# Rows of the attention mix loaded during the sample turns, into tiles of their own and into the places of cached keys

## The chip, the cores and the metric

One core of one Trainium2 chip runs the whole kernel. The metric is device time in microseconds (us) of one execution; smaller is better. The median of three runs of the kernel before is 1789.62 us (1786.05 to 1790.71).

## The reference

One layer of a streaming encoder, for a prompt of 1024 rows (T) and a sample of 64 rows (S) that share the weights; the width is 1024. Cut to what matters here:

```
h  = rms_norm(x, g_norm1);  q, k, v, forget logits = h @ w_in        # 16 heads: 8 of kind A, 8 of kind B
oa, ob = attend(prompt heads), attend(sample heads with cached k, v)
x  = x + concatenate([oa, ob]) @ w_o                                 # the "mix" times w_o
mk, mv = memory keys and values = rms_norm(mem) @ w_mkv
x  = x + attend(rms_norm(x) @ w_mq, mk, mv) @ w_mo
x  = x + conv_ffn(rms_norm(x))                                       # w_up, conv, silu, w_down
```

Products run as three products of parts: each f32 operand is split into a high part (`hi`, a cast on ScalarE) and a low part (`lo`, the difference, on VectorE or GpSimd), and hi\*hi, lo\*hi and hi\*lo are summed in PSUM.

## The kernel before, in words

**Prompt attention.** Heads go in pairs, eight of them. Each finished block of 256 query rows of a pair is written to the DRAM tensor `mixd` (eight rows of 128 x 1024, one for each pair; 512 KB each). The last of these writes goes out at 601 us.

**Memory and sample, beside each other.** The list `line` holds pieces of the memory product (L679, 24 matmuls for one half of a column block; weights `mwraw` are loaded by L661 and split by L668/L669 into `mwhi` and `mwlo`). Between its pieces stand the sample's eight turns, one for each pair of heads, in the order SAMPLES = 4, 7, 5, 6, 0, 1, 3, 2. A turn of a pair consists of:
- `load`: queries and new keys `sqd` (L727), values `svn` (L729), the bias `s`, two tiles of cached keys `kraw` (L740, three places in all) and of cached values `vraw`;
- `prep`: four transposes on TensorE (L754), from which ScalarE and VectorE make queries `sq` and new keys `skn` (L265 and L266, two each, by turns);
- `splitk`: `kchi` (L774, ScalarE) and `kclo` (L775, VectorE);
- `score`: matmuls L797 (cached keys) and L798 (new keys), then VectorE adds the bias and takes the largest value (L800, L802, L807), ScalarE takes the exponential (L808), VectorE the reciprocal of the sum (L810);
- `turn` and `sum`: transposes of the probabilities (L822), split into `pth` (L823) and `ptl` (L824), and ten products with the values (L835);
- the end: two halves `st` (L842, ScalarE) and `su` (L843, VectorE), a transpose of `su` (L847), and two copies into `smix` (L849).

The turns overlap: the loads, `prep` and `splitk` of the next turn stand beside the score of this one and the sums of the last one. The list PER says how many memory pieces go with each turn. The last two turns are those of pair 3 (the seventh) and of pair 2 (the eighth).

**Output projection.** After the seventh turn the memory pieces are used up, and `open_left` opens new pools on the left side: `raw`, `hi` and `lo` for the weights w_o (loads L911, splits L919 and L920), and `ha`, the eight rows of the mix as parts. Row k is loaded into `mraw` (L976), cast on ScalarE (L979) and differenced on VectorE (L980); the sample's columns come from `smix` (L1022, L1023). A pool `stage` has four places for `mraw`: four rows are loaded at once, and the split of row k loads row k + 4. The product with w_o (L937) takes the rows in order, k = 0 to 7, three matmuls each; the first two products (chunks of 384 columns into `pj`) share the first weight tiles, and the third begins with `PT`.

**What sets the order.** The program is written as one list of steps (`weave` puts small steps between large ones), but the compiler of the tile framework then orders each engine's instructions by its own planning. Engines execute their queues strictly in that order. All DMAs are issued by SyncE's queue (SP), in order too: a load that waits for its place holds up all those behind it.

Of the kernel before, what the change touches and what calls it, by code (L numbers as in the profile page):

```python
# [7 lines left out]
F32 = mybir.dt.float32  # L8
F32R = mybir.dt.float32r
ACT = mybir.ActivationFunctionType  # L10
ALU = mybir.AluOpType
# [4 lines left out]
P = 128  # L16
T = 1024
# [3 lines left out]
KT = 8  # L21
# [4 lines left out]
SLOW = 7  # L26
LEFT = (0, 0, 0, 15)
PER = (4, 8, 9, 12, 6, 5, 6, 0, 0)
STAGE, MIXES = 4, 8
WARM = 20  # L30
EPS = 1e-6
NEG = -1e30
# [9 lines left out]
def hybrid_step(ctx: ExitStack, tc: tile.TileContext, i: dict, o: dict):  # L42
    nc = tc.nc
    act, dve, pool, pe = nc.scalar, nc.vector, nc.gpsimd, nc.tensor

    def f32(ap):
        return ap.bitcast(F32)
# [17 lines left out]
    mixd = dram.tile([8, P, T], F32, name="mixd")  # L65
# [38 lines left out]
    left = ExitStack()  # L104
# [540 lines left out]
    left = ExitStack()  # L645
# [241 lines left out]
    rest = ExitStack()  # L887
# [2 lines left out]
    zq = [mq.tile([P, 4, S], F32R, name=f"sq{x}") for x in range(2)]  # L890
    for x in range(2):
        pool.memset(f32(zq[x][:, 1:3]), 0.0)
    samples = [Sample(p) for p in SAMPLES]
    samples[0].load()
    step(0, [samples[0].prep, lambda: samples[0].splitk(0), lambda: samples[0].splitk(1)])
# [59 lines left out]
    mixr = []  # L955
# [6 lines left out]
    def open_left():  # L962
        nonlocal stream
        left.close()
        stream = Stream(late_left.enter_context(tc.tile_pool(name="wr", bufs=1, side="left")))
        x = late_left.enter_context(tc.tile_pool(name="x0", bufs=1, side="left")).tile([P, 384], F32, name="x0")
        nc.sync.dma_start(x, i["xT"][0, :, 0:384])
        ha = mixes.enter_context(tc.tile_pool(name="ha", bufs=1, side="left"))
        stage = rest.enter_context(tc.tile_pool(name="stage", bufs=1, side="left"))
        mixr.extend(parts(ha, "a"))  # L970
        stream.fetch()
        raws = {}

        def load_mix(k):
            raws[k] = stage.tile([P, T], F32, name="mraw", bufs=STAGE)
            nc.sync.dma_start(raws[k], mixd[k])  # L976

        def split_mix(k):
            act.copy(mixr[0][k][:, 0:T], raws[k])  # L979
            dve.tensor_tensor(mixr[1][k][:, 0:T], raws[k], f32(mixr[0][k][:, 0:T]), op=ALU.subtract)  # L980

        for k in range(STAGE):
            load_mix(k)

        def split_load(k):
            split_mix(k)
            if k + STAGE < KT:
                load_mix(k + STAGE)

        return ha, [lambda k=k: split_load(k) for k in range(KT)], x  # L990

    old, mixes_todo, ha = [], [], None
    todo = first[:]
    for x in range(len(samples) + 1):
        if not line and ha is None:
            ha, mixes_todo, early_x = open_left()
        cur = samples[x] if x < len(samples) else None
        nxt = samples[x + 1] if x + 1 < len(samples) else None
        if nxt:
            nxt.load()  # L1000
        new, fin = [], []
        if cur:
            new = [cur.score, cur.splitv]
        if nxt:
            fin = [nxt.prep, lambda: nxt.splitk(0), lambda: nxt.splitk(1)]
        subs = new[:1] + old[:2] + new[1:] + old[2:-1] + fin[:1] + old[-1:] + fin[1:]
        main = line[:PER[x]]
        del line[:PER[x]]
        if ha and not mixes_todo:
            stream.upto(4)  # L1010
            if todo:
                main = todo.pop(0).pieces
        subs += mixes_todo[:MIXES]
        del mixes_todo[:MIXES]
        weave(main, subs)
        if cur:
            c = cur.nc
            old = [lambda z=z, u=cur: u.turn(z) for z in range(2)] + [lambda u=cur: u.sum(0)]
            old += ([lambda u=cur: u.turn(2), lambda u=cur: u.sum(1)] if c == 2 else [])
            old += [lambda u=cur, c=c: u.sum(c), cur.out]  # L1020
# [844 lines left out]
```

## Time and profile before

| what | value |
|---|---|
| median of three runs | 1789.62 us (1786.05 to 1790.71) |
| the profiled execution, its own time | 1791.44 us |
| its span, first to last instruction | 1789.7 us |
| TensorE (PE) busy | 1717.8 us, 96% |
| VectorE (DVE), ScalarE (ACT), GpSimd (POOL) busy | 1208.6, 937.0, 644.7 us |
| mean DMA rate over the span | 112 GB/s |
| chain that ended last, in TensorE | 49% of the span in its largest groups |

Times in the profile count from the first instruction. PE is the matmuls, PEld the weight loads beside them, SPq the queue of SyncE. A row of the timeline gives the start, the duration (for "x3" of three together), the engine, the line, what is written from what, and in brackets the idle time of that engine before it with the one that ended it. A row of the stages gives the stage, its length, the busy time of each engine with its count, the granted TensorE clock as a share of full speed, the share of DMA engines in use, and GB/s.

### The profile page before, as it was taken

The page shows a single profiled execution, that of the slowest core. Times are in us where ns is not written, and L with a number is a line of the kernel's source. Part 1 is how long each engine was busy: PE and PEld are TensorE (multiplying, and loading weights), DVE is VectorE, ACT ScalarE, POOL GpSimd, SP SyncE. Part 2 cuts the span into 40 slices and gives each one's busy share as a digit, 9 for nine tenths or more (in the row PEclk, how much of TensorE's full clock was granted, in tenths as well). Part 3 has the DMA queues.
Part 4 walks back from the last instruction along what each step waited for, and adds up shares of the span by engine and source line. Part 5 has one row for each costly group of instructions (what it writes and reads, how often), then busy time and mean ns, then how long its engine had stood idle before and what let it go on. Part 6 is the DMA issues. An engine that isn't in the chain of part 4 may idle for free.

```text
span 1789.7 us, 33957 instructions
## 1 busy us (share of the span) xinstructions
PE 1717.8 (96%) x12432; PEld 1667.2 (93%) x12432; DVE 1208.6 (68%) x2642; ACT 937.0 (52%) x2058; POOL 644.7 (36%) x931
## 2 busy tenths in 40 slices
PE   7898999999997898999999999999999999999999
PEld 6888999999997787999999999999999999999999
DVE  5767667677677777433444379877777777677994
ACT  6756666677677577334545455433333333433332
POOL 4656657878777443453433612000000000000000
PEclk8999999999999999999999999999999999999999
DMA  7322122122113677441111563222222222884232
GB/s 248 98 63 66 57 73 80 51 73 75 47 56 106 203 248 234 155 144 54 54 48 57 165 204 102 79 76 87 83 87 74 73 73 73 272 296 158 77 118 80
DMA packets 134247, 199.87 MB, mean 112 GB/s; under 512 B 20968, under 2 KB 74088, under 8 KB 134080
## 3 DMA queue, kind: packets, MB, share of 16 engines
q1 hardware_dynamic: 134080, 197.70, 34.9%
q8 instruction: 98, 1.61, 0.4%
q14 instruction: 69, 0.57, 0.1%
HBM read 155.35 MB, written 45.44 MB: 112 GB/s over the span
## 4 chain that ended last, share of the span: by engine, by line
PE 49%; DVE 2%; issue 1%; POOL 1%; DMA 1%; ACT 0%; SPq 0%; POOLq 0%; ACTq 0%; DVEq 0%
PE W L1449 25%; PE W L1746 12%; PE pj L937 7%; PE W L937 1%; PE S L1192 1%; PE tq L1228 1%; PE O L1228 1%; POOL lo L920 1%; DMA kvraw<-in_w_down_dram 1%; PE PT L1215 0%; DMA f<-x2d 0%; PE O L1192 0%; PE PT L1173 0%; POOL s L1207 0%; ACT hi L919 0%
## 5 line engine op out<-in xcount | busy, mean ns | idle before, releaser
L299 PE MATMUL pj<-whi,xhi 128*128 128x384 f32 (+1 forms) x512 | 195.5, 382 | 2.7 <-DVE flog L314 1.6
L299 PE MATMUL pj<-wlo,xhi 128*128 128x384 f32 (+1 forms) x512 | 176.4, 344 | 4.5 <-POOL wlo L123 4.5
L299 PE MATMUL pj<-whi,xlo 128*128 128x384 f32 (+1 forms) x512 | 175.2, 343 | 0.6 <-DVE xlo L131 0.6
L1555 POOL COPY s<-gp 128x2 f32<-128x2 f32 x22 | 15.8, 718 | 335.8 <-DVE gp L1554 335.8
L1449 PE MATMUL W<-h,hi 128*128 128x272 f32 x704 | 134.4, 288 | 1.4 <-ACT qlo L1585 1.4
L504 ACT ACTIVATE s<-s,mx 128x640 f32<-128x640 f32 (+7 forms) x128 | 94.4, 737 | 77.6 <-DVE mx L502 76.7
L1746 PE MATMUL W<-f,hi 128*128 128x272 f32 x672 | 127.6, 287 | 3.6 <-DVE f L1314 2.3
L541 DVE TENSOR_TENSOR ptl<-PT,pth 128x512 fp32r<-128x512 f32 (+2 forms) x192 | 99.5, 522 | 38.5 <-ACT pth L540 36.2
L1449 PEld LDWEIGHTS W<-h,hi 128*128 128x128 f32 x704 | 110.8, 188 | 1.7 <-ACT qlo L1585 1.6
L1746 PEld LDWEIGHTS W<-f,hi 128*128 128x128 f32 x672 | 105.3, 188 | 4.4 <-DVE f L1314 2.5
L540 ACT CAST pth<-PT 128x512 fp32r<-128x512 f32 (+2 forms) x192 | 84.7, 448 | 43.9 <-PE PT L539 42.3
L299 PEld LDWEIGHTS pj<-wlo,xhi 128*128 128x128 f32 x512 | 99.2, 194 | 6.3 <-POOL wlo L123 6.1
L299 PEld LDWEIGHTS pj<-whi,xhi 128*128 128x128 f32 x512 | 98.8, 193 | 4.8 <-DVE flog L314 1.9
L1449 PE MATMUL W<-h,lo 128*128 128x272 f32 x352 | 101.8, 289 | 0.0
L1313 ACT CAST hi<-raw 128x512 fp32r<-128x512 f32 x68 | 42.2, 621 | 109.5 <-PE W L1449 59.2
L299 PEld LDWEIGHTS pj<-whi,xlo 128*128 128x128 f32 x512 | 97.6, 191 | 1.8 <-DVE xlo L131 1.6
L539 PE MATMUL PT<-ident,s 128*128 128x128 f32 x528 | 90.6, 278 | 7.8 <-DVE ptl L541 7.3
L1746 PE MATMUL W<-f,lo 128*128 128x272 f32 x336 | 96.7, 288 | 0.0
L499 PE MATMUL S<-kh,q 128*128 128x256 f32 (+1 forms) x304 | 77.6, 280 | 12.2 <-DVE mx L502 12.0
L937 PE MATMUL pj<-a,hi 128*128 128x384 f32 (+1 forms) x352 | 88.8, 335 | 0.2 <-ACT hi L919 0.2
L507 POOL TENSOR_SCALAR s<-s,ssum 128x640 f32<-128x640 f32 (+6 forms) x96 | 70.3, 734 | 48.6 <-DVE ssum L505 36.5
L554 PE MATMUL O<-pth,v 128*128 128x256 f32 (+1 forms) x304 | 78.1, 281 | 8.3 <-ACT mhi L265 7.6
(551 smaller groups left out, 6038.1 us busy)
## 6 DMA issues: line engine op xcount, KB each, us to landing
raw<-in_w_down_dram SPq DMA_DIRECT2D x45, 256.0 KB, 3.6
wraw<-in_w_dram SPq DMA_DIRECT2D x56, 192.0 KB, 2.4
raw<-in_w_up_dram SPq DMA_DIRECT2D x41, 256.0 KB, 2.8
h<-ad SPq DMA_DIRECT2D x32, 272.0 KB, 5.0
mwraw<-in_w_mkv_dram SPq DMA_DIRECT2D x16, 512.0 KB, 5.9
raw<-in_w_mo_dram SPq DMA_DIRECT2D x32, 256.0 KB, 3.4
kvraw<-in_w_down_dram SPq DMA_DIRECT2D x32, 256.0 KB, 3.2
ad<-t SPq DMA_DIRECT2D x22, 272.0 KB, 2.3
```

The source lines that it names most:

```text
L299: pe.matmul(pj[:, :nw], x2[a][:, k, t * P:(t + 1) * P], wt[k][b][:, :nw], start=n == 0, stop=n == 3 * KT - 1)
L499: pe.matmul(sp[:, a:a + (k1 - k0) * P], q, kk[:, h, src], start=m == 0, stop=m == 1)
L504: act.activation(s[:, :n], s[:, :n], ACT.Exp, bias=mx, scale=-1.0, accum_out=sm)
L507: pool.tensor_scalar(s[:, :n], s[:, :n], sm, 1.0, op0=ALU.mult, op1=ALU.mult)
L539: pe.transpose(pt[:, b - ch[0]], self.s[j][:, (b - w0) * P:(b - w0 + 1) * P], ident)
L540: act.copy(hi[:, f:f + n, j], pt[:, f:f + n])
L541: dve.tensor_tensor(lo[:, f:f + n, j], pt[:, f:f + n], f32(hi[:, f:f + n, j]), op=ALU.subtract)
L554: pe.matmul(op[:, cols], groups[p, b // 2].v[:, b % 2, h].rearrange("p a d -> p (a d)"), pt[:, x, cols], start=b == self.full[0] and m == ...
L937: pe.matmul(out()[:, :cn], w[a][:, k % 4], x[b][k][:, c0:c0 + cn], start=k == 0 and n == 0, stop=k == KT - 1 and n == 2)
L1313: act.copy(hi, t)
L1449: pe.matmul(w[:, z, :Q], a(p, j), rights[j][b][:, z * Q:z * Q + Q], start=fresh and begin and j == 0 and x == 0, stop=final and end and j ...
L1746: pe.matmul(ws[m][:, z, :Q], la[p][:, m * P:(m + 1) * P], ra[b][:, z * Q:z * Q + Q], start=first and y == 0 and what in opening, stop=fina ...
```

## The change

The pool `stage` and its four places go. Four `mraw` places are opened in `mq`, the pool of the sample's tiles. Rows 0 and 1 are loaded in turn 4 (counted from 0), behind the loads for the turn that follows, rows 2 and 3 in turn 5 likewise. When the left pools open, three more rows (4, 5, 6) are loaded into places of `kraw`, the cached keys, as these come free; the split of row 0 loads row 7 into an `mraw` place. What is computed stays the same.

```diff
-STAGE, MIXES = 4, 8
+MIXED, MIXES = (4, 5), 8
...
+    mraws = []
+
+    def load_mix(tag="mraw"):
+        k = len(mraws)
+        mraws.append(mq.tile([P, T], F32, name=tag, bufs={"mraw": 4, "kraw": 3}[tag]))
+        nc.sync.dma_start(mraws[k], mixd[k])
+
     samples = [Sample(p) for p in SAMPLES]
...
-        stage = rest.enter_context(tc.tile_pool(name="stage", bufs=1, side="left"))
         mixr.extend(parts(ha, "a"))
         stream.fetch()
-        raws = {}
-
-        def load_mix(k):
-            raws[k] = stage.tile([P, T], F32, name="mraw", bufs=STAGE)
-            nc.sync.dma_start(raws[k], mixd[k])
 
         def split_mix(k):
-            act.copy(mixr[0][k][:, 0:T], raws[k])
-            dve.tensor_tensor(mixr[1][k][:, 0:T], raws[k], f32(mixr[0][k][:, 0:T]), op=ALU.subtract)
-
-        for k in range(STAGE):
-            load_mix(k)
-
-        def split_load(k):
-            split_mix(k)
-            if k + STAGE < KT:
-                load_mix(k + STAGE)
-
-        return ha, [lambda k=k: split_load(k) for k in range(KT)], x
+            act.copy(mixr[0][k][:, 0:T], mraws[k])
+            dve.tensor_tensor(mixr[1][k][:, 0:T], mraws[k], f32(mixr[0][k][:, 0:T]), op=ALU.subtract)
+            if len(mraws) < KT:
+                load_mix()
+
+        for k in range(3):
+            load_mix("kraw")
+
+        return ha, [lambda k=k: split_mix(k) for k in range(KT)], x
...
         if nxt:
             nxt.load()
+        if x in MIXED:
+            load_mix()
+            load_mix()
```

The framework plans the queues anew, and the order moves far beyond the loads. Two places matter for what follows. In the change the line numbers behind the edit are higher by 1 to 7: L937 is L944 there, L919 is L926, L979 is L980.

First TensorE, from the last matmul of the memory product on. `sqd` is the input of the last turn's `prep`, `s_10190` and `s_10194` are the probabilities of the seventh turn, `kchi_10444` and `kchi_10452` the last turn's keys, `su` the end of a turn. Before:

```order
L754 MATMUL tq_10419<-ident_61,sqd_10321 128x64 x4
...
L679 MATMUL pj_10371<-mwhi_10236,mlo_8601 128x256
L847 MATMUL PT_10440<-ident_61,su_10411 64x128
L822 MATMUL PT_10515<-ident_61,s_10190 128x128 x4
L822 MATMUL PT_10524<-ident_61,s_10190 64x128
L798 MATMUL tq_10499<-skn0_10424,sq1_9095 128x64
...
L797 MATMUL S_10498<-kchi_10444,sq1_9095 128x512
...
L835 MATMUL O_10533<-vc_10384,pth_10516 128x256
...
L835 MATMUL O_10533<-svh_10289,ptl_10526 128x256
L847 MATMUL PT_10550<-ident_61,su_10545 64x128
```

The same place in the changed kernel:

```order
L679 MATMUL pj_10379<-mwhi_10244,mlo_8601 128x256
L847 MATMUL PT_10448<-ident_61,su_10419 64x128
L822 MATMUL PT_10518<-ident_61,s_10194 128x128 x4
L822 MATMUL PT_10527<-ident_61,s_10194 64x128
L835 MATMUL O_10536<-vc_10392,pth_10519 128x256
L754 MATMUL tq_10427<-ident_61,sqd_10329 128x64 x4
...
L835 MATMUL O_10536<-svh_10297,ptl_10529 128x256
L798 MATMUL tq_10502<-skn0_10432,sq1_9095 128x64
...
L847 MATMUL PT_10553<-ident_61,su_10548 64x128
L797 MATMUL S_10501<-kchi_10452,sq1_9095 128x512
```

The last turn's transposes L754 stood ahead of the last memory piece and now stand behind the seventh turn's probabilities, and the last turn's scores L797 now stand behind the whole sum of the seventh turn and the transpose of its `su`; before, they were mixed with that sum.

Second ScalarE, from the last turn's cached values on. `s_10325` and `s_10333` are the exponential of the last turn's scores, `a0k` the high part of row k of the mix, `hi` the first weights of w_o. Before:

```order
L782 CAST vc_10530<-vraw_10332 128x8x64
L979 CAST a00_10467<-mraw_10489 128x1024
L808 ACTIVATE s_10325,ssum_10511<-s_10325,mx_10510 128x576
L842 ACTIVATE st_10544<-O_10533,ssum_10358 64x64
L979 CAST a01_10468<-mraw_10491 128x1024
L842 ACTIVATE st_10544<-O_10533,ssum_10358 64x64
L979 CAST a02_10469<-mraw_10493 128x1024
L979 CAST a03_10470<-mraw_10495 128x1024
L849 COPY smix_9093<-PT_10550 64x64 x2
L919 CAST hi_10578<-raw_10483 128x512
```

The same place in the changed kernel:

```order
L849 COPY smix_9093<-PT_10553 64x64
L774 CAST kchi_10456<-kraw_10338 128x512
L782 CAST vc_10533<-vraw_10340 128x8x64
L808 ACTIVATE s_10333,ssum_10514<-s_10333,mx_10513 128x576
L980 CAST a00_10472<-mraw_10036 128x1024
L980 CAST a01_10473<-mraw_10038 128x1024
L980 CAST a02_10474<-mraw_10203 128x1024
L980 CAST a03_10475<-mraw_10205 128x1024
L980 CAST a04_10476<-kraw_10494 128x1024
L980 CAST a05_10477<-kraw_10496 128x1024
L926 CAST hi_10575<-raw_10488 128x512
```

Before, one row's cast stood ahead of the exponential and three between it and the first weights, with the seventh turn's `st` halves among them. Now that end of the seventh turn is over before the exponential, and six rows' casts stand between the exponential and the first weights.

## The prediction

> **What bounds the kernel now.** I read the stages first, then the timeline of each engine around the place where the change works.
>
> ```profile
> core 0: us, PE busy (x) PEld busy (x) DVE busy (x) ACT busy (x) POOL busy (x), PEclk, DMA share, GB/s
> 698.00:709.00 11.00, 6.34 (x33) 4.07 (x31) 8.68 (x19) 9.70 (x22) 1.45 (x1) 0.94 0.74 237
> 709.00:722.60 13.60, 12.94 (x60) 11.74 (x61) 10.68 (x20) 8.35 (x21) 6.28 (x4) 0.80 0.51 171
> 722.60:790.00 67.40, 67.40 (x410) 67.40 (x410) 22.67 (x37) 25.93 (x50) 33.56 (x29) 1.00 0.51 160
> ```
>
> From 722.6 us on TensorE is busy without a break, so whatever moves 722.6, the start of the third w_o product, moves the end by as much. Ahead of it lie eleven microseconds in which TensorE has little to do (6.34 busy) and ScalarE is nearly full (9.70). The TensorE timeline of that stretch, and of what leads to it:
>
> ```profile
> 696.86 0.40 PE L754 MATMUL tq<-ident,sqd 64*128 64x64 f32 x4
> ...
> 697.89 0.28 PE L679 MATMUL pj<-mwhi,mlo 128*128 128x256 f32 x1
> 698.49 0.27 PE L847 MATMUL PT<-ident,su 128*64 128x128 f32 x1 [0.32 <-DVE su L843]
> 698.73 0.87 PE L822 MATMUL PT<-ident,s 128*128 128x128 f32 x5
> ...
> 701.88 0.28 PE L835 MATMUL O<-vc,pth 128*128 128x256 f32 x1
> 702.00 0.28 PE L835 MATMUL O<-vc,ptl 128*128 128x256 f32 x1
> ...
> 702.90 0.28 PE L835 MATMUL O<-svh,ptl 64*128 64x256 f32 x1
> 707.21 0.27 PE L847 MATMUL PT<-ident,su 128*64 128x128 f32 x1 [4.03 <-DVE su L843]
> 707.45 1.31 PE L822 MATMUL PT<-ident,s 128*128 128x128 f32 x5
> 708.98 1.01 PE L937 MATMUL pj<-a,hi 128*128 128x384 f32 x2 [0.22 <-ACT hi L919]
> 710.64 0.69 PE L937 MATMUL pj<-a,lo 128*128 128x384 f32 x1 [0.66 <-POOL lo L920]
> ...
> 714.22 0.63 PE L937 MATMUL pj<-a,hi 128*128 128x384 f32 x2
> ...
> 722.59 0.51 PE L937 MATMUL PT<-a,hi 128*128 128x384 f32 x2
> ```
>
> One idle time stands out: 4.03 us before the seventh turn's `su` is transposed. Why `su` was late stands in VectorE's timeline:
>
> ```profile
> 701.27 0.68 DVE L775 TENSOR_TENSOR kclo<-kraw,kchi 128x512 fp32r<-128x512 f32 x1
> ...
> 702.55 0.69 DVE L800 CUSTOM_DVE_ANT_0 s<-S,s 128x512 f32<-128x512 f32 x1 [0.41 <-PE S L797]
> ...
> 703.29 0.16 DVE L807 TENSOR_TENSOR mx<-smx 128x1 f32<-128x1 f32 x1
> ...
> 704.77 0.26 DVE L843 SCALAR_TENSOR_TENSOR su<-O,ssum,st 64x64 f32<-64x64 f32 x1
> 705.52 1.23 DVE L980 TENSOR_TENSOR a<-mraw,a 128x1024 fp32r<-128x1024 f32 x1 [0.48 <-ACT a L979]
> 706.78 0.29 DVE L843 SCALAR_TENSOR_TENSOR su<-O,ssum,st 64x64 f32<-64x64 f32 x1
> ```
>
> The two halves of `su` have a 1.23 us split of a mix row between them. So the early mix splits cost this idle time; but the first w_o product (708.98) waited for something else, the cast of its weights on ScalarE:
>
> ```profile
> 698.58 0.36 ACT L265 ACTIVATE skn<-tq,gd 128x128 fp32r<-128x128 f32 x1
> ...
> 699.27 0.62 ACT L774 CAST kchi<-kraw 128x512 fp32r<-128x512 f32 x1
> 699.79 0.58 ACT L823 CAST pth<-PT 128x512 fp32r<-128x512 f32 x1
> ...
> 701.47 1.05 ACT L979 CAST a<-mraw 128x1024 fp32r<-128x1024 f32 x1
> 703.48 0.78 ACT L808 ACTIVATE s<-s,mx 128x576 f32<-128x576 f32 x1 [0.96 <-DVE mx L807]
> 704.16 0.19 ACT L808 ACTIVATION_READ_ACCUMULATOR s<-s,mx 128x1 f32 x1
> ...
> 705.84 1.99 ACT L979 CAST a<-mraw 128x1024 fp32r<-128x1024 f32 x2
> ...
> 708.31 1.66 ACT L919 CAST hi<-raw 128x512 fp32r<-128x512 f32 x3
> ```
>
> The chain that sets 722.6 is thus: last memory matmul (697.89), last turn's exponential (703.48, 5.59 later), first weights' cast, first product (708.98, 5.50 later), third product (722.59, 13.61 later). The loads of the mix rows are in none of these steps. The change moves loads, and with them the planned order; I cost the order.
>
> **The change, part by part.** *From the last memory matmul to the last exponential.* Before, the last turn's L754 began at 696.86, ahead of that matmul, and its scores ran between the seventh turn's sums. In the new order the same steps stand one behind the other. Counted from the last memory matmul: the sixth turn's second half of `su` now stands behind the seventh turn's exponential (0.78 and 0.19) and reciprocal, so its transpose comes at about 1.5 instead of 0.6. The first O product needs five L822 (0.87) and `pth` (0.58); L754 stands behind it and ends at 3.5. `sq` and `skn`, each a pass on ScalarE and one on VectorE, four passes of some 0.36 with hand-overs, take 1.85: 5.4. The two halves of `st` and `su`, four passes of 0.3 behind `skn`, with their transpose (0.27) and one copy into `smix`, put the first `kchi` at 6.85. Two `kchi` of 0.62 with the other copy between them: 8.2. `kclo` 0.68, the last L797 some 0.4, L800 0.69 and L807 0.16: with hand-overs the exponential starts at 10.4, against 5.6. That is +4.8 us. I take a hand-over at 0.1 us; at nothing the sum is +3.5, and at 0.2 (the brackets show up to 0.48) it is +6.0.
>
> *From the exponential to the first product.* Before, 5.50 us. Now six casts stand ahead of the weights. A cast can start 0.78 behind the exponential's start; two take 1.99 where one takes 1.05, so a further one adds 0.95: 0.78 + 5 x 0.95 + 1.05 = 6.6, and the product starts 0.67 behind its weights' cast (708.31 to 708.98): 7.25, or +1.7. The idle 4.03 us goes, since `su` has no mix split in its way, but TensorE then waits longer for these casts. Late next is the weights' low part:
>
> ```profile
> 709.06 5.00 POOL L920 TENSOR_TENSOR lo<-raw,hi 128x512 fp32r<-128x512 f32 x3 [5.96 <-ACT hi L919]
> ```
>
> It needs 5.00 / 3 = 1.67, and the product's third matmul waits for it (0.66) as before.
>
> *From the first to the third product.* Here the early rows could help: rows 4 to 7 were cast late, and the planner mixed two products to bridge that. But what stretched these 13.61 us was the slow matmul: the pair at 708.98 takes 1.01, that at 714.22 0.63, that at 722.59 0.51, in a stage with a clock of 0.80. It follows an idle time of 4.03 us; the new order has one of about 5 us (from the last five L822, done 2 us behind the exponential, to 7.25). The VectorE chain of seven differences (1.23 each, from 2 us behind the exponential) stays ahead of the slow matmuls. So 13.6 again, within 0.4 either way.
>
> The Trainium skill (TensorE: Matmul & The Clock Gate, Part 1) has the array at half clock after an idle window of about 3.4 us and at full clock after about 3.4 us of sustained work. The trace has the slow pairs from 707.21 to about 714.2, 7 us, twice that; by the page's figure the stretch would be some 2 us shorter.
>
> *The loads.* What is removed, added or moved on SP, with the weight cast that is nearest to its limit:
>
> ```profile
> 577.01 1.38 SPq L976 DMA_DIRECT2D mraw<-mixd  x3
> ...
> 675.23 0.84 SPq L661 DMA_DIRECT2D mwraw<-in_w_mkv_dram  x2
> ...
> 701.80 1.38 SPq L911 DMA_DIRECT2D raw<-in_w_o_dram  x3
> ```
>
> ```profile
> 682.21 1.14 ACT L668 CAST mwhi<-mwraw 128x512 fp32r<-128x512 f32 x2 [0.40 <-DMA mwraw<-in_w_mkv_dram]
> ```
>
> Three rows that went out at 577 now go out with a fourth in the sixth and seventh turn, the first two directly ahead of the last memory weights. That is 1 MB more in front of them; at the 237 GB/s of the stage above it is up to 4.2 us. The cast already waited 0.40 for its load. In the new order the next sums stand between, and these casts come some 3.5 us later by themselves; so the delay of the second weight tile costs 0 to 1.2 us, I take 0.6. Rows 4 to 6 wait for `kraw` places: the second for the last turn's first `kclo`, shortly before the last exponential, and SP's queue holds the three w_o loads (701.80 before) behind it, to about 1.5 us before that exponential. Their cast comes 6.6 behind it, so some 8 us cover a load; row 7 waits for row 0's difference and is covered by six casts. I cost these waits at nothing.
>
> *The first turns.* With the three rows gone from 577, SP reaches the first turn's second key tile ahead of a store that it stood behind:
>
> ```profile
> 620.91 1.14 ACT L774 CAST kchi<-kraw 128x512 fp32r<-128x512 f32 x2 [2.00 <-DMA kraw<-in_cbk_dram]
> ...
> 626.83 0.88 PE L822 MATMUL PT<-ident,s 128*128 128x128 f32 x6 [0.91 <-ACT s L808]
> ...
> 633.49 0.39 PE L679 MATMUL pj<-mwlo,mhi 128*128 128x256 f32 x1 [0.97 <-DVE mx L807]
> ```
>
> ScalarE waited 2.00 us for that tile, and TensorE 0.91 and 0.97 in the scores that follow. At best both go, -1.9; at worst nothing; I take -0.8, since the second turn's loads stay where they are.
>
> *Sum:* +4.8 + 1.7 + 0 + 0.6 - 0.8 = **+6.3 us**; with all low ends +2.9, with all high ends +9.3. The profiled execution takes 1791.44 us, 1.7 over its span, and 1.8 more than the median of 1789.62. Against the median the sum gives 1795.9 us.
>
> **The rivals.** *The old overlap holds* (not slower). The last exponential stays near 5.6 us behind the last memory matmul, because the steps that I add up one behind the other find their inputs ready. For it: ScalarE is the only engine near full there, and it loses the casts that stood in this place (701.47, 705.84). Against it: queues are strict, and in the new one both `kchi` stand behind the copies of the seventh turn's end. Then +1.7 - 0.8 = +0.9, 1790.5 us; with the 0.91 and 0.97 both gone, -0.2. It decides if the exponential comes less than 2 us later than before.
>
> *Loads bound the first product* (slower than my sum). The w_o loads go out five to six us later than before, with three mix rows of 512 KB around them: 1.5 MB and the weights' 0.75 MB at 237 GB/s are 9.5 us against my cover of 8. Then the product starts some 2 us later: 1797.9 us. For it: the stages' DMA share of 0.74. Against it: only one mix row of the three can stand directly ahead of the weights.
>
> *The slow clock ends earlier.* If the matmuls are slow for half as long as the 7 us of the trace, 3.5 us at twice the pace are saved by half: -1.8, and the third product begins that much earlier: 1794.1 us. That is the page's rule; against it stand the slow pairs above, behind an idle time like the new one.
>
> That the change does nothing but move loads, with no gain at all, is excluded by the order; the first rival covers it in time.
>
> **How the numbers follow.** My forecast gets 0.55, the old overlap 0.22, the loads 0.12, the clock 0.11. About 0.3% (5.4 us, 1784.3 to 1795.0) is what a measurement of this kernel can tell from no change. The forecast's own range of +2.9 to +9.3 lies mostly above that bound, so two thirds of its 0.55 go to slower (0.37) and 0.18 to same; the overlap gives 0.18 to same and 0.04 to faster; the loads go to slower (0.12); the clock gives 0.08 to same and 0.03 to slower. Sum: faster 0.04, same 0.44, slower 0.52. The range takes in the overlap at -0.2 with 0.9 for what I read off by hand, and the high end of the sum: 1788.5 to 1799.0 us.
>
> **What would show it.** The profile after should have no 4 us of idle time before the seventh turn's L847, but one of about 5 us before the first L944, ended by ScalarE's `hi`, with slow matmuls behind it; the last exponential some 10 us behind the last memory matmul; the first product some 7 us behind the exponential. I am wrong if the exponential comes within 7.5 us, if `hi` waits for its DMA, or if TensorE is slow for less than 5 us.

## The result and the profile after

The changed kernel takes 1792.84 us (median of 15 runs, 1790.56 to 1797.90), the kernel before 1788.51 us (15 runs, 1784.22 to 1792.02). The ratio is 1.0025, 95% interval [1.0017, 1.0033], so 3.0 to 5.9 us slower. The forecast was 1795.9 us, 6.3 slower than the median that was known then, with a range of 1788.5 to 1799.0.

The two profiled executions can't be laid over each other from the start of the span. The first matmul of the memory product (the first L679) comes 3.03 us earlier in the trace of the change, and in the traces of the ten other kernels below it lies anywhere between 594.77 and 599.64 us: executions differ by that much ahead of the place where the change works. All places below are therefore counted from the first L679 of the same trace. Of before, TensorE's first memory matmul, the first turn's exponential on ScalarE, the last turn's `ptl` on VectorE, and TensorE's transpose of the last turn's `su`:

```profile
598.65 0.28 PE L679 MATMUL pj<-mwhi,mhi 128*128 128x256 f32 x1
```

```profile
625.48 1.20 ACT L808 ACTIVATE s<-s,mx 128x1088 f32<-128x1088 f32 x1 [1.03 <-DMA kraw<-in_cbk_dram]
```

```profile
712.95 0.69 DVE L824 TENSOR_TENSOR ptl<-PT,pth 128x512 fp32r<-128x512 f32 x1
```

```profile
720.73 0.27 PE L847 MATMUL PT<-ident,su 128*64 128x128 f32 x1
```

The stages of the change, cut at its last memory matmul's end, its last exponential, its first and its third w_o product:

```profile
core 0: us, PE busy (x) PEld busy (x) DVE busy (x) ACT busy (x) POOL busy (x), PEclk, DMA share, GB/s
692.04:702.91 10.87, 6.35 (x30) 3.94 (x29) 5.26 (x16) 5.65 (x17) 1.73 (x2) 0.87 0.60 192
702.91:710.02 7.11, 1.33 (x5) 0.88 (x6) 5.43 (x6) 7.11 (x10) 0.00 (x0) 0.50 0.80 292
710.02:724.39 14.37, 13.57 (x59) 12.03 (x60) 11.33 (x21) 7.53 (x22) 8.21 (x4) 0.75 0.35 107
724.39:790.00 65.61, 65.61 (x400) 65.61 (x400) 22.28 (x34) 25.14 (x48) 32.89 (x29) 1.00 0.48 149
```

As before, TensorE has no break behind the third product, so that product still sets the end. In the second stage ScalarE is busy throughout (7.11 of 7.11) and TensorE hardly (1.33). TensorE's timeline:

```profile
595.62 0.28 PE L679 MATMUL pj<-mwhi,mhi 128*128 128x256 f32 x1
...
691.76 0.28 PE L679 MATMUL pj<-mwhi,mlo 128*128 128x256 f32 x1
693.05 0.27 PE L847 MATMUL PT<-ident,su 128*64 128x128 f32 x1 [1.00 <-DVE su L843]
...
695.02 0.46 PE L754 MATMUL tq<-ident,sqd 64*128 64x64 f32 x4
...
699.56 0.49 PE L797 MATMUL S<-kchi,sq 128*128 128x512 f32 x1 [0.94 <-ACT kchi L774]
700.28 0.79 PE L797 MATMUL S<-kclo,sq 128*128 128x512 f32 x1 [0.23 <-DVE kclo L775]
...
703.83 1.33 PE L822 MATMUL PT<-ident,s 128*128 128x128 f32 x5 [1.89 <-ACT s L808]
710.02 1.01 PE L944 MATMUL pj<-a,hi 128*128 128x384 f32 x2 [4.86 <-ACT hi L926]
...
715.61 0.58 PE L835 MATMUL O<-vc,ptl 128*128 128x256 f32 x1
...
720.08 0.27 PE L847 MATMUL PT<-ident,su 128*64 128x128 f32 x1
...
724.39 0.51 PE L944 MATMUL PT<-a,hi 128*128 128x384 f32 x2
```

The 4.03 us ahead of the seventh turn's L847 are gone (1.00 is left); 4.86 us stand ahead of the first w_o product, ended by ScalarE's `hi`. ScalarE's own rows show what it did meanwhile, and that its exponential had waited for VectorE:

```profile
619.92 1.21 ACT L808 ACTIVATE s<-s,mx 128x1088 f32<-128x1088 f32 x1
...
698.89 0.62 ACT L774 CAST kchi<-kraw 128x512 fp32r<-128x512 f32 x1
...
702.91 0.77 ACT L808 ACTIVATE s<-s,mx 128x576 f32<-128x576 f32 x1 [2.02 <-DVE mx L807]
703.69 3.87 ACT L980 CAST a<-mraw 128x1024 fp32r<-128x1024 f32 x4
707.46 1.99 ACT L980 CAST a<-kraw 128x1024 fp32r<-128x1024 f32 x2
709.36 1.66 ACT L926 CAST hi<-raw 128x512 fp32r<-128x512 f32 x3
```

VectorE has seven differences ahead of the last turn's `ptl`, and behind that the last row's difference and those of the sample's columns ahead of the second half of the last `su`:

```profile
704.75 4.63 DVE L981 TENSOR_TENSOR a<-mraw,a 128x1024 fp32r<-128x1024 f32 x4 [0.77 <-DMA raw<-in_w_o_dram]
709.30 5.66 DVE L981 TENSOR_TENSOR a<-kraw,a 128x1024 fp32r<-128x1024 f32 x3
714.88 0.68 DVE L824 TENSOR_TENSOR ptl<-PT,pth 128x512 fp32r<-128x512 f32 x1
...
719.64 0.29 DVE L843 SCALAR_TENSOR_TENSOR su<-O,ssum,st 64x64 f32<-64x64 f32 x1 [0.25 <-ACT st L842]
```

So two queues end together here. TensorE is busy for 13.57 of the 14.37 us up to the third product. On VectorE that `su` is done at 719.93, 17.02 us behind the exponential (16.64 before), its transpose L847 starts at 720.08, and in the new order 4.31 us of w_o products stand between L847 and the third product (1.86 before: 720.73 to 722.59). With this order the third product can't start before this `su` is done and those products have run, some 21.4 us behind the exponential, however early TensorE is with the rest; it starts 21.48 behind it.

Worked out from these rows and their like in every trace, in us behind the first L679:

| kernel | first exponential | last memory matmul | last exponential | first product | third product | ratio, 95% interval |
|---|---|---|---|---|---|---|
| before | 26.83 | 99.24 | 104.83 | 110.33 | 123.94 | |
| the change | 24.30 | 96.14 | 107.29 | 114.40 | 128.77 | 1.0025 [1.0017, 1.0033] |
| e1 late order back | 24.59 | 99.03 | 104.61 | 110.10 | 123.56 | 0.9998 [0.9986, 1.0010] |
| e2 rows late | 24.65 | 96.81 | 103.37 | 111.93 | 125.76 | 1.0010 [1.0001, 1.0019] |
| e3 weights first | 24.01 | 95.85 | 107.00 | 111.13 | 133.09 | 1.0052 [1.0037, 1.0067] |
| e4 warm | 24.00 | 95.85 | 108.56 | 115.68 | 130.75 | 1.0040 [1.0025, 1.0055] |
| e5 rows behind weights | 24.19 | 100.75 | 108.04 | 113.54 | 127.29 | 0.9991 [0.9982, 1.0000] |
| e6 last turn early | 23.99 | 95.85 | 107.13 | 114.24 | 128.63 | 1.0023 [1.0013, 1.0033] |
| e7 both | 24.52 | 96.38 | 107.56 | 114.68 | 130.60 | 1.0042 [1.0030, 1.0055] |
| e8 two rows ahead | 24.68 | 97.12 | 109.68 | 114.89 | 129.45 | 1.0029 [1.0017, 1.0040] |
| e8 again | 24.65 | 97.11 | 109.25 | 114.46 | 129.02 | 1.0022 [1.0013, 1.0030] |
| e9 exponential's part back | 24.63 | 97.72 | 103.29 | 111.96 | 126.25 | 1.0022 [1.0013, 1.0031] |
| e10 rows behind the weight loads | 24.65 | 97.23 | 102.81 | 108.31 | 122.06 | 1.0003 [0.9991, 1.0016] |

By these columns the change loses 4.83 us (128.77 less 123.94): -3.10 up to the last memory matmul, +5.56 from there to the exponential, +1.61 to the first product, +0.76 to the third. The medians differ by 4.33. A trace is one execution and the ratio is of many, so where the two disagree the ratio decides.

### The profile page after: what moved, and what is told of

Same layout as the page of the kernel before. It is cut to its first block, busy times and chain, and to the rows that moved or that the text cites. A ratio compares the mean times of both kernels' runs of the same rounds, so it can differ in the third digit from the quotient of the medians.

```text
span 1791.4 us, 33961 instructions
## 1 busy us (share of the span) xinstructions
PE 1716.0 (96%) x12432; PEld 1666.6 (93%) x12432; DVE 1209.3 (68%) x2642; ACT 937.6 (52%) x2058; POOL 649.1 (36%) x931
## 3 DMA queue, kind: packets, MB, share of 16 engines
q8 instruction: 98, 1.61, 0.4%
## 4 chain that ended last, share of the span: by engine, by line
PE 74%; DVE 8%; ACT 6%; POOL 4%; issue 4%; DMA 4%; SPq 0%; POOLq 0%; DVEq 0%; ACTq 0%
PE W L1450 25%; PE pj L944 12%; PE W L1747 11%; PE pj L299 10%; PE O L554 3%; PE PT L539 2%; PE S L499 2%; DVE s L502 1%; PE W L944 1%; PE pj L679 1%; ACT s L504 1%; PE tq L326 1%; PE S L1193 1%; PE tq L1229 1%; PE O L1229 1%
## 5 line engine op out<-in xcount | busy, mean ns | idle before, releaser
L944 PE MATMUL pj<-a,hi 128*128 128x384 f32 (+1 forms) x352 | 88.5, 334 | 4.9 <-ACT hi L926 4.9
```

The source lines that it names most:

```text
L944: pe.matmul(out()[:, :cn], w[a][:, k % 4], x[b][k][:, c0:c0 + cn], start=k == 0 and n == 0, stop=k == KT - 1 and n == 2)
```

## The experiments

The theory going in was that of the prediction: the planned order around the last turns costs the time, the loads do not. The rival: the loads themselves cost it, since rows of the mix now stand among the last turns' keys and in the places of cached keys.

**The late order put back (e1).** All loads and tiles of the change stay; ordering edges without any wait put four queues, from the seventh turn's last memory pieces to the first products, in the order that the kernel before has there (the table holds places in program order, as that kernel queues them).

```diff
+TABLE = {"PE": (...), "Activation": (...), "DVE": (...), "Pool": (...)}
+def listed(tc, table):
+    ...
+        for a, b in zip(mine, mine[1:]):
+            tc.add_manual_dep(b, a.name, NoSync, reason="listed")
     in_order(tc, ramp)
+    listed(tc, TABLE)
```

> The changed kernel with all its loads and tiles, but from the seventh turn's last memory pieces to the first w_o products the queues of TensorE, ScalarE, VectorE and GpSimd stand in the order of the kernel before. My theory (the planned order there costs the time, the loads do not, and the first turns are 2 us shorter): the last exponential comes about 5.6 us behind the last memory matmul instead of 11.2, the first product about 5.5 behind it, and the time is 1 to 3 us under the kernel before (ratio about 0.999). Rival (the loads cost it: mix rows among the last turns' keys, and w_o loads held behind kraw places): the time stays about 4 us above the kernel before (ratio 1.002 to 1.003), and casts of keys, rows or weights wait for their DMAs.

The ratio is 0.9998 [0.9986, 1.0010]: the loss is gone, and the 1 to 3 us of gain did not come. The trace shows both. The exponential stands 5.58 behind the last memory matmul and the third product 18.95 behind the exponential, as before. But the last memory weights now wait for their loads, first on ScalarE in this run, then the same casts in the change, which waited for nothing:

```profile
680.32 1.14 ACT L668 CAST mwhi<-mwraw 128x512 fp32r<-128x512 f32 x2 [2.38 <-DMA mwraw<-in_w_mkv_dram]
683.05 0.62 ACT L668 CAST mwhi<-mwraw 128x512 fp32r<-128x512 f32 x1 [0.82 <-DMA mwraw<-in_w_mkv_dram]
```

```profile
679.95 1.15 ACT L668 CAST mwhi<-mwraw 128x512 fp32r<-128x512 f32 x2
...
681.34 1.13 ACT L668 CAST mwhi<-mwraw 128x512 fp32r<-128x512 f32 x2
```

The first turns' gain (2.24 at the first exponential) is 0.21 at the last memory matmul. So the order is the cause of the loss, shown; and the loads alone are worth nothing that can be measured. In this trace they take back at these weights what they give early; the last run takes that wait away. With the order the long slow stretch of TensorE (17.0 us in the change, last section) is gone too, 6.8 us in this trace (705.3 to 712.1); what of the loss ahead of the exponential is clock and what is steps in a row was not tried apart.

**The rows late (e2).** The stage and four places of the kernel before, and the order of the run above in all four engines; only the loads differ.

```diff
         if nxt:
-            nxt.load()
+            got = nxt.load()
+            if x == 4:
+                behind.append(got)
...
-        for k in range(STAGE):
-            load_mix(k)
+        with tc.issue_after(behind[0].ins):
+            for k in range(STAGE):
+                load_mix(k)
```

> The kernel before with its stage and four places, the rows' loads held behind the loads of the turn after the fifth, and the same order of all four engines as in the run above. My theory (the first turns gain because no rows go out at 577, and it does not matter when the first rows are loaded as long as they are there): the first exponential about 24.3 us behind the first memory matmul as in the changed kernel (26.8 before), and the time as in the run above, 1 to 3 us under the kernel before. Rival (the gain comes from the rows being loaded among the turns into tiles of their own): the rows' casts wait for their loads, and the time is that of the kernel before or 1 to 4 us above.

In SP's queue the rows then came behind the last turn's keys, later than I had meant. The first exponential is at 24.65 and the last memory matmul at 96.81: the first turns gain with the old tiles too, once no row goes out at 577 us, and without rows ahead of the last weights the gain is still there at the end of the memory product. Then the second row is missing, and the casts stop for it:

```profile
704.71 1.04 ACT L980 CAST a<-mraw 128x1024 fp32r<-128x1024 f32 x1 [2.77 <-DMA mraw<-mixd]
```

Ratio 1.0010 [1.0001, 1.0019]. Loaded as late as here the rows hold up the casts, as the rival said; a time between was not tried with these tiles. The tiles of their own are not needed for the first turns' gain, as the theory said.

**The weights first (e3).** The change's order, but on ScalarE:

```diff
 L980 CAST a00<-mraw
+L926 CAST hi<-raw
 L980 CAST a01<-mraw
 L980 CAST a02<-mraw
+L926 CAST hi<-raw
 L980 CAST a03<-mraw
 L980 CAST a04<-kraw
 L980 CAST a05<-kraw
-L926 CAST hi<-raw x3
+L926 CAST hi<-raw
```

> The changed kernel in its own order, but on ScalarE the first three casts of w_o stand behind the first, third and fourth row's cast instead of behind the sixth. My theory (the casts in front of the weights hold the first product): the first product comes about 2.6 us behind the last exponential instead of 7.1, the third product 2 to 4 us earlier, and the time is 0 to 2 us above the kernel before (ratio about 1.0007). Rival (the differences on VectorE or the last turn's sum bound the third product): the first product comes earlier, TensorE waits behind it, and the time stays at a ratio of 1.002 to 1.003.

It is slower than the change: 1.0052 [1.0037, 1.0067]. First on ScalarE, VectorE and TensorE in this run:

```profile
707.58 0.62 ACT L926 CAST hi<-raw 128x512 fp32r<-128x512 f32 x1 [1.64 <-DMA raw<-in_w_o_dram]
```

```profile
709.17 4.88 DVE L981 TENSOR_TENSOR a<-mraw,a 128x1024 fp32r<-128x1024 f32 x3 [1.99 <-ACT a L980]
```

```profile
720.26 0.58 PE L835 MATMUL O<-vc,ptl 128*128 128x256 f32 x1 [4.23 <-DVE ptl L824]
```

The weights' load had not landed, so the cast behind them came late, VectorE's differences behind that, and `ptl` behind those. Two things follow. The six casts of the change cover a load that lands late, the rival of the prediction that the loads bound the first product: it landed some 3.5 us behind the exponential (704.12 to 707.58), and the change's weights cast starts 6.45 behind it. And the first product is not all that bounds the third: it came 3.27 earlier than in the change (111.13 and 114.40), the third 4.32 later. TensorE's path from the exponential by the first to the third product has VectorE's queue, seven differences and then `ptl`, as a second bound beside it.

**TensorE kept warm (e4).** Twenty transposes of the identity into an unused bank, behind the last turn's transposes:

```diff
             stream.upto(4)
+            warm = ps.tile([P, 2, 512], F32, name="S", bufs=1)
+            for n in range(20):
+                pe.transpose(warm[:, 0, n % 4 * P:n % 4 * P + P], ident, ident)
```

> The changed kernel in its own order with 20 transposes of the identity on TensorE between the last turn's transposes and the first w_o product, into a bank that nobody reads, so that the idle 4.9 us are filled. Clock theory (the matmuls behind the wait are slow because TensorE had idled): pairs of products take 0.51 us from the first on instead of 0.84 to 1.01, the stretch from the first to the third product is 11.0 to 12.0 instead of 14.4 us, and the time 2 to 3 us under the changed kernel (ratio to before about 1.001). Rival (the slow phase lasts as long as it does whatever TensorE has done just before, or VectorE's differences bound): ratio 1.002 to 1.003.

```profile
710.24 3.30 PE L1014 MATMUL S<-ident 128*128 128x128 f32 x20
715.32 0.62 PE L944 MATMUL pj<-a,hi 128*128 128x384 f32 x2 [1.77 <-ACT hi L926]
...
720.91 0.39 PE L835 MATMUL O<-vc,ptl 128*128 128x256 f32 x1 [1.80 <-DVE ptl L824]
...
723.23 1.01 PE L944 MATMUL pj<-a,hi 128*128 128x384 f32 x2
```

The first products are fast (0.62 for a pair instead of 1.01), and it gains nothing: TensorE now waits 1.80 for `ptl`, and a slow pair of 1.01 comes behind that wait. Ratio 1.0040 [1.0025, 1.0055]. My clock theory, that the slow matmuls cost 2 to 3 us in the end, fell: their slowness lay in the shadow of VectorE's queue, whose last `su` is done 17.01 us behind the exponential, as in the change. That the third product is 1.98 later than in the change is only in part the transposes' doing: in this trace the exponential ahead of them is 1.27 later (108.56).

**The rows one turn later (e5).** The first run of the study with

```diff
-MIXED, MIXES = (4, 5), 8
+MIXED, MIXES = (5, 6), 8
```

> The first run of this study (the changed kernel with the queues of the kernel before around the last turns) with the four early rows one turn later: two behind the last memory weights, two behind the last turn's keys. There the last weights' casts waited 2.38 and 0.82 us for loads that stood behind two rows. Theory (the first turns gain 2 us, and rows ahead of the last memory weights take it away again): these waits fall under 0.6, the third product starts 121.5 to 122.5 us behind the first memory matmul (123.9 before), and the time is 1.5 to 3 us under the kernel before (ratio about 0.9985). Rival (the rows come too late then, as in the run where all of them were late): casts of rows wait for their loads, ratio 1.000 to 1.001.

Ratio 0.9991 [0.9982, 1.0000]. The weights' waits are gone, as expected, but the first row's cast got a wait of its own, for the last store of memory values:

```profile
704.39 1.04 ACT L980 CAST a<-mraw 128x1024 fp32r<-128x1024 f32 x1 [2.66 <-DMA vmd<-kv]
```

The first row's parts lie in the places of the memory product's pool, which come free with that store; its queue now has two rows ahead of it, and the cast starts 5.1 us behind that store's issue (699.25) instead of some 2.4 (699.09 to 701.47 before). This execution also had a slow stretch of TensorE at 631 us that stands behind its 100.75 for the last memory matmul (last section), so its columns can't be compared; by the ratio alone it is at or a little under the kernel before.

**The last turn early, without and with the warm transposes (e6, e7).** On ScalarE `pth` behind the first w_o cast, on VectorE `ptl` behind five differences:

```diff
 L981 a04<-kraw,a04
+L824 ptl<-PT,pth x2
 L981 a05<-kraw,a05
 L981 a06<-kraw,a06
-L824 ptl<-PT,pth
 L981 a07<-mraw,a07
-L824 ptl<-PT,pth
```

> The changed kernel with the last turn's probabilities split earlier: pth behind the first w_o cast on ScalarE, ptl behind five differences on VectorE instead of seven. Theory (two bounds of the same length stand behind the last exponential: slow matmuls on TensorE, and on VectorE the row differences ahead of ptl; TensorE had no wait in the changed kernel's trace, so it alone sets the third product there): ptl some 3 us earlier, the third product and the time as in the changed kernel (ratio 1.002 to 1.003). Rival (VectorE alone bounds): third product 2 us or more earlier, ratio about 1.001.

> The run above with 28 transposes of the identity on TensorE ahead of the first w_o product (20 alone gave full speed to the first products, but TensorE then waited 1.80 for ptl). Theory of the two bounds: with both taken away the stretch from the first to the third product falls from 14.4 to 11 to 12.5 us, the time 2 to 3 us under the changed kernel (ratio 1.001 or below). Rival (the slow phase is only moved, and comes back behind the next waits): the stretch stays at 13.5 or above, ratio 1.002 to 1.004.

Alone it changes nothing, 1.0023 [1.0013, 1.0033], with the third product where it was (128.63), though `ptl` starts 7.57 us behind the exponential instead of 11.97: the last `su` is done at 17.03, as in the change. With 28 warm transposes it is 1.0042 [1.0030, 1.0055], and the stretch from the first to the third product 15.92 us instead of 14.37. First TensorE, then VectorE of the second of these runs:

```profile
722.38 0.27 PE L847 MATMUL PT<-ident,su 128*64 128x128 f32 x1 [2.23 <-DVE su L843]
```

```profile
717.18 2.30 DVE L981 TENSOR_TENSOR a<-mraw,a 128x1024 fp32r<-128x1024 f32 x1
```

TensorE passes `ptl` now and waits for `su`, which stands on VectorE behind the last row's difference and those of the sample's columns and is done 17.03 us behind the exponential once more. So of the two bounds the one on TensorE went, and the one on VectorE was never shortened: moving `ptl` ahead of two differences leaves all eight ahead of `su`. The products behind L847 then take 5.86 us instead of 4.31, since TensorE's next slow stretch (3.4 us, last section) falls on them. So the rival holds: the slow phase moved behind the next wait. That both bounds have the same length, as I had put it, is true; that `ptl` is where VectorE's ends is not.

**Two rows ahead of the exponential (e8, two times).** On ScalarE the casts of rows 0 and 1 ahead of the last L808, on VectorE the first difference ahead of L810.

```diff
+L980 CAST a00<-mraw
+L980 CAST a01<-mraw
 L808 ACTIVATE s<-s,mx
-L980 CAST a00<-mraw
-L980 CAST a01<-mraw
```

> The changed kernel with two rows' casts ahead of the last exponential, where ScalarE idled 2.02 us, and the first row's difference ahead of the reciprocal on VectorE. Theory (what stands on ScalarE and VectorE between the last exponential and the first product and ptl costs one for one): the exponential stays at 107.3 us behind the first memory matmul, the first product comes 1.9 earlier, the third 1.7 to 2.2 earlier (21.5 behind the exponential becomes 19.5), and the time is about 2 us under the changed kernel (ratio 1.0010 to 1.0017). Rival (what the planned order lost up to the exponential is all, and the rest is hidden): ratio 1.002 to 1.003.

> The kernel with two rows' casts ahead of the last exponential once more, since its trace had slow matmuls from 696.6 us on (699.5 in the changed kernel), which made the exponential 2.4 us late. If that was this one execution: exponential at 107 to 107.5 us behind the first memory matmul, third product 127 to 127.5 (128.8 in the change), ratio 1.0010 to 1.0017. If it belongs to the order: exponential at 109 or later again, ratio 1.002 to 1.003.

Both traces have the third product 19.77 behind the exponential (21.48 in the change), as expected: with one difference moved ahead of the reciprocal the last `su` is done at 15.31 instead of 17.02, and the third product follows one for one. But both have the exponential 2.0 to 2.4 later than in the change; the ratios, 1.0029 [1.0017, 1.0040] and 1.0022 [1.0013, 1.0030], show no gain. By the second expectation this "belongs to the order", but nothing ahead of the exponential except the two casts was moved, and it started right behind VectorE's largest value, not behind them. Some 1.0 us of the delay is there at the last memory matmul already (97.12 and 97.11 against 96.14). The rest goes with the clock: TensorE's slow stretch sets in at 696.6 and 699.0 us, 3.3 and 4.0 us behind the last memory matmul (8.3 in the change). The four other runs with the change's order up to the exponential fit: with the stretch 3.0 (e4), 5.8 (e6), 7.9 (e3) and 8.8 us (e7) behind that matmul the exponential comes 12.71, 11.28, 11.15 and 11.18 behind it, in the two traces here 12.56 and 12.14, in the change 11.15. The place of the stretch differs between the two executions of this kernel too, so that of one trace need not hold for the medians. Why the 1.7 us do not show in the time stays open; the second ratio's interval has room for the 1.0013 to 1.0017 that were expected.

**Only the exponential's part back (e9).** By edges as in the first run, the order of before up to the last exponential, and behind it six casts ahead of `hi` and seven differences ahead of `ptl`, as in the change.

> The changed kernel with the queues of the kernel before up to the last exponential only; behind it stand, as in the change, six rows' casts ahead of the w_o weights on ScalarE and seven differences ahead of ptl on VectorE (with the seventh turn's st and su directly behind the exponential). Theory (both parts of the order cost, one after the other): the exponential 5.6 us behind the last memory matmul, the third product 21 to 22.5 behind the exponential (19.0 with the old order there, 21.5 in the change), and a time 2 to 3 us above the first run of this study, ratio 1.0008 to 1.0018. Rival (only the part up to the exponential costs; what stands behind it is covered, as two runs suggest in which less work there did not shorten the time): third product 19 to 19.5 behind the exponential, ratio 1.0000.

The exponential stands 5.57 behind the last memory matmul, as expected, and the third product 22.96 behind the exponential, a little above the forecast. The first w_o product waited for `hi` again:

```profile
708.34 1.01 PE L944 MATMUL pj<-a,hi 128*128 128x384 f32 x2 [2.12 <-ACT hi L926]
```

Ratio 1.0022 [1.0013, 1.0031]. The rival falls: the order behind the exponential costs time when the exponential is early. By the traces it costs 2.7 of the 5.2 us between the first run and the change (123.56, 126.25, 128.77), by the ratios nearly all (0.9998, 1.0022, 1.0025); the intervals don't settle the division.

**The rows behind the weight loads (e10).** The first run of the study with the pairs of rows loaded at the end of their turn:

```diff
-        if x in MIXED:
-            load_mix()
-            load_mix()
...
         weave(main, subs)
+        if x in MIXED:
+            load_mix()
+            load_mix()
```

> The first run of this study with one thing changed: the two pairs of rows stand on SP behind the two weight loads, or stores, of their turn instead of ahead of them. Theory (rows ahead of the last memory weights took 1.9 us of the 2.1 that the first turns gain): the casts of these weights wait about 0.4 us (2.38 and 0.82), the third product starts 121.5 to 122 us behind the first memory matmul, ratio 0.9985 to 0.9992. Rival (the DMA queues are full there, whatever stands first): keys or rows wait instead, third product at 123 or later, ratio 0.9995 to 1.0005.

The trace does what was expected: no cast of the last weights waits, the last memory matmul is at 97.23 instead of 99.03 and the third product at 122.06, 1.88 earlier than before. The ratio does not show it: 1.0003 [0.9991, 1.0016], where 0.9989 was worth expecting from 1.88 us; that lies just outside the interval. Three runs with the late order of before and early rows give 0.9998, 0.9991 and 1.0003, so no version here beats the kernel before by more than a measurement can tell, and that the wait at the last weights is what hid the first turns' gain is not shown by the times.

## Why the prediction was right, and where it was not

*The cause* was right, and it is shown: the planned order around the last turns, not the loads. With the order put back the loss is gone.

*From the last memory matmul to the last exponential:* 11.15 us, forecast 10.4; +5.56, forecast +4.8. The chain is the one that was added up: L754 behind the O product, the two `kchi` with the copies between them, each step waiting for the one ahead of it. Some 0.3 us of the 0.75 that the sum lacked is there at the first `kchi`, 7.13 behind the last memory matmul for 6.85: the passes that the sum names for that step (four of 0.3, 0.27, and a copy of 0.2) make 1.67 us, and it took 1.45 for them. What it did not have either is that the matmuls at its end became slow: the clock fell at 700.1 us, and the L797 behind the first `kclo` takes 0.79 and the last one 0.65, where some 0.4 had been used.

*From the exponential to the first product:* 7.11, forecast 7.25. Six casts, then the weights, as said. The cover of "some 8 us" for the w_o loads held: with the casts taken away (e3) the weights' cast waited 1.64, and the load had then landed some 3 us ahead of the place where that cast stands in the change.

*From the first to the third product:* 14.37, forecast 13.6 within 0.4; the term is +0.76 instead of 0. The idle time came (4.86) and slow matmuls behind it, but not the one by the other: TensorE had been at half clock since 700.1 us, ahead of the exponential and of the idle time. It stayed so until 717.1, 7.1 us into this part (5.4 before: 708.98 to 714.4). That the slow time came out near the forecast was luck. That VectorE's differences stay ahead of the slow matmuls was wrong: seven of them were put at 1.23 each, 8.6 us, and took 4.63 + 5.66 = 10.29. `ptl` behind them is ready at 715.56, just when TensorE needs it (715.61), and the last `su` behind that holds the third product as long as TensorE's own work does. The runs with warm transposes show both as waits.

*The loads and the first turns* are where the sum was mis-sized. I took -0.8 of at most -1.9 for the first turns; the first exponential comes 2.53 earlier, and the gain lies beyond the end that I had called the best case, in all traces without the rows at 577 us (23.99 to 24.68 against 26.83). I took +0.6 for rows ahead of the last memory weights; in the change these casts wait for nothing, as the sentence on their later place said, and with the old order the price is 1.8 us (99.03 less 97.23), above the 1.2 that I had as the end. The rest of the -3.10, 0.57, fits work that now stands behind the last memory matmul, the last turn's L754 (0.40 before) among it, which the prediction had counted in the exponential's part but not taken off here.

So the forecast of +6.3 was 1.5 us too high by the trace (+4.83) and 2.0 by the medians (+4.33): 2.9 too high ahead of the last memory matmul (-0.2 for -3.10), and 0.8 too low in each of two parts behind it. That errors of both signs left the sum nearer than its terms is luck. *The old overlap holds* did not come: the exponential is 11.15 behind the last memory matmul, and 2.46 later counted from the first L679, where the rival had less than 2. *Loads bound the first product* did not, in the change; it stood right behind the casts. *The slow clock ends earlier* did not: it lasted 17.0 us, 7.1 of them behind the first product, not 3.5.

## What to carry to other kernels

A load that is moved to an earlier time lets a planner move everything that hung on it; cost the new order on each engine before the loads, and put the old order back by edges to tell the two apart. When a wait is filled or taken away, ask what is ready just behind it on the other engines, and follow each queue to its last hand-over: here TensorE's products and VectorE's queue up to the last `su` ended together, and four runs (e3, e4, e6, e7) that left that `su` where it was, or made it later, gained nothing. A load that is well hidden may still stand ahead of one that is not: in the trace, rows ahead of the last weights gave back what the first turns had won.

## What the runs showed of the hardware

TensorE's slow stretches come in whole pieces of about 3.4 us, and a wholly idle time ahead of them is not needed. Five such stretches, each with the 3.40 us ahead of it: of before, of the change, of e7, of e5 and of e6.

```profile
704.20:707.60 3.40, 0.39 (x3) 0.29 (x4) 2.85 (x6) 3.35 (x7) 0.00 (x0) 1.00 0.93 337
707.60:714.40 6.80, 5.92 (x19) 4.77 (x19) 5.28 (x5) 6.71 (x17) 5.00 (x3) 0.50 0.87 290
```

```profile
696.70:700.10 3.40, 1.64 (x8) 0.85 (x7) 1.71 (x6) 1.99 (x6) 0.00 (x0) 1.00 0.57 169
700.10:717.10 17.00, 9.28 (x28) 7.04 (x29) 14.19 (x16) 13.07 (x25) 8.27 (x5) 0.50 0.53 183
```

```profile
719.90:723.30 3.40, 1.17 (x8) 0.95 (x7) 2.27 (x11) 0.88 (x4) 0.71 (x1) 1.00 0.34 118
723.30:726.70 3.40, 3.40 (x13) 3.40 (x12) 1.48 (x4) 1.44 (x4) 0.00 (x0) 0.50 0.49 144
```

```profile
627.90:631.30 3.40, 1.80 (x14) 1.42 (x13) 2.88 (x6) 2.66 (x6) 1.73 (x3) 1.00 0.98 296
631.30:641.50 10.20, 10.20 (x40) 8.75 (x41) 5.91 (x19) 5.71 (x19) 3.65 (x3) 0.50 0.49 170
```

```profile
693.10:696.50 3.40, 2.56 (x17) 2.07 (x18) 2.01 (x6) 2.10 (x6) 0.46 (x1) 0.99 0.46 99
696.50:717.00 20.50, 11.78 (x37) 8.63 (x36) 16.15 (x21) 14.75 (x29) 9.11 (x5) 0.50 0.52 184
```

The granted clock (the third number from the end) is half over 6.8, 17.0, 3.4, 10.2 and 20.5 us: two, five, one, three and six times 3.4. The Trainium skill (TensorE: Matmul & The Clock Gate, Part 1) has free-running windows of 3413 ns, which agrees. It has the clock fall after an idle window and come back after a busy one; these rows differ in both: TensorE was busy for 1.64, 1.80 or 2.56 of the 3.40 us ahead of a slow stretch, and in e5 it stayed slow for three windows with 10.20 of 10.20 us busy. The stretch at 631 us fell on one execution alone, in the middle of the memory product, where the same queue in other traces ran at full clock: half of 10.2 us is 5.1 us of clock, beside 7.8 us between the fastest and the slowest execution of the kernel before. Executions with a lower mean clock tend to be the slower ones (correlation -0.51 over the 25 executions of the kernel before that were timed beside e5, -0.85 over the 12 of e5); how much of the scatter such stretches make up was not tried. That the change has more slow time is not so in its profiled execution alone: the mean granted clock is 0.9877 over the 15 executions of the change and 0.9901 over those 25 of before.

A difference of 128 x 1024 on VectorE takes 4.63 / 4 = 1.16 us while GpSimd is idle, and 5.66 / 3 = 1.89 in the stage in which GpSimd splits weights (8.21 us busy there, 0.00 in the stage ahead of it); in e7 one takes 2.30. In a sum of queued differences beside such splits the larger figure is the one to use.
